# A hybrid attention and recurrence block: attention's output projection as seven block products, the gates' input sums by accumulating transfers, and fill work moved

## The chip, the cores and the metric

The kernel runs on one core of a Trainium2 chip. A core has five engines that run side by side and meet at semaphores: TensorE (PE in the profile; its weight loads are PEld), VectorE (DVE), ScalarE (ACT), GpSimd (POOL) and SyncE (SP). SP, ACT and POOL also issue transfers, each on a queue of its own (q1, q10 and q0 in the profile), which 16 DMA engines carry out. The metric is the time of one execution in device microseconds; lower is better.

## The reference

One layer of an encoder on x, 1024 tokens by 1024 channels, in float32:

```python
xn = rmsnorm(x, norm1_g)
u = xn @ w_in                                   # 1024 x 5632
q_sb, k_sb, v_sb, f_raw, i_hg, q_hg, g_hg, gate_sb, gate_hg = split(u)
o_sb = stick_breaking_attention(q_sb, k_sb, v_sb)      # 8 heads of 64: 512 wide
o_hg = hgrn2(silu(q_hg), (1 - lb) * sigmoid(-f_raw), i_hg, log_f)   # 4 heads of 128: 512 wide
o_hg = rmsnorm(o_hg, hg_norm_g) * silu(g_hg)
merged = sigmoid(gate_sb + b) * (o_sb @ w_o_sb) + sigmoid(gate_hg + b2) * (o_hg @ w_o_hg)
h = x + merged @ w_out
h = h + square(relu(rmsnorm(h, norm2_g) @ w_ff1)) @ w_ff2
out = rmsnorm(h, final_g)
```

The change is about `o_sb @ w_o_sb` (1024 x 512 by 512 x 1024) and about the operands of the products that give `gate_sb`, `gate_hg` and `g_hg`.

## The kernel before

*Products.* A float32 operand is split into a high part and a low part: `hi_lo` casts the high part on ScalarE (line 156) and subtracts on VectorE for the low part (line 161). A product is then three matmuls (`three`, line 570): high by high, high by low, low by high. Most matmuls have 512 columns.

*Seven products for eight.* The gates' projection, `w_out` and the MLP are multiplied as two-by-two blocks in Winograd's way: seven block products of sums of blocks in place of eight of the blocks themselves. The gates need their input xn in four blocks, whole (not split), added and subtracted, and each sum split again. `whole_input` (line 1455) makes a block whole in place, with an accumulating transfer on POOL's queue: low part += high part, 512 KB each. `sum_forms` (line 1461) then builds the sums for products 5, 6, 7 and 3 with additions on VectorE and splits them.

*Order of the work.* Each engine runs its instructions in one order that is fixed when the program is built. A planner makes that order: among the instructions that its own clock says are ready, it takes the one that stands first in the program, so an instruction can be issued well ahead of its place in the code. Buffers are handed out in the same way. Three things are written by hand. TensorE has two lanes: the main lane (attention's or the recurrence's own small products) and the fill lane (large projections, held as jobs in a stream `st`); a fill product may run at most two main blocks ahead (`open_block`, line 110). `st.advance` says how many steps of fill, six matmuls each, follow each piece of main work. And SP's loads are one chain in program order (`load`, line 135).

*The stages around the change.*

1. Attention, 64 items (8 heads x 8 query blocks). Fill: the projections of the heads, two raw jobs, and some of the recurrence's `f` and `q` projections, up to the job `j_att`. POOL's queue meanwhile builds sums of blocks of `w_out` in DRAM (`out_weight_sums`, line 1337). A finished head's output goes to DRAM (`od`).
2. The recurrence, four heads. `hg_levels` (line 1073) has 8 pieces a head, `hg_tail` (line 1214) 6; the tail of one head runs beside the levels of the next. Fill, so many steps a piece as `FILL` says (line 2434): the rest of the projections, then eight raw jobs (`raw_job`, line 1399, seven steps each) that compute, for each block of 128 gate columns, the two products of the gates that need no sums of xn, and load attention's output again (`osr`).
3. Attention's output projection, `sb_job` (line 1505): four jobs of two column blocks. For a column block and a token half, eight k-and-part products in 12 matmuls accumulate in one PSUM bank; the first half is multiplied by its gate, both are stored to `yd`. The first three jobs run beside the end of the recurrence and step `sum_forms` along; the fourth is held back and runs inside the first gate pair.
4. The gates, `gates` (line 1751): ten `GatePair`s, two of them for `g_hg`. Each runs `x6`, `y5`, `x7`, `y3`, four block products into two banks.

*Buffers.* 40 slots of 512 KB (`slot`), 10 of 256 KB (`half`), eight PSUM banks (`bank`), and of each of the weights' raw, high and low tiles two (`wpool`).

Of the kernel before, what the change touches and what calls it, by code (L numbers as in the profile page):

```python
# [2 lines left out]

# [36 lines left out]
def kernel(  # L40
# [972 lines left out]
    def silu_epilogue(h, key):  # L1013
        def ep(ps, half):
            t = hg_slot(h, key, half)
            ps, t = of_half(ps, half), as_half(t, half)
            nc.scalar.activation(t, ps, AF.Sigmoid)
            if h < 2:
                x = as_half(slot_n(f"qx{h}_{half}", 512), half)
                nc.scalar.copy(x, ps)  # L1020
                owed_wlo.append(lambda: mul(t, x, t))
                return
            mul(t, ps, t)

        return ep
# [282 lines left out]
    a_sb, a_hg = Split("asb"), Split("ahg")  # L1308
# [144 lines left out]
    WAIT = 7  # L1453
# [7 lines left out]
    def sum_forms():  # L1461


        raw = whole
        def split(m, kp, src):
            forms[m, kp] = tuple(slot(f"gs{n}{m}{kp}", F32R) for n in "hl")
            hi_lo(*forms[m, kp], src)

        for j in range(2):
            whole_input(0, j)  # L1470
        yield from range(WAIT)
        s1, s2 = {}, {}
        for kp in range(2):
            s1[kp] = slot(f"gs1{kp}")
            ins = add(s1[kp], raw[1, 0, kp], raw[1, 1, kp])
            if kp == 0:
                after(ins, hg_sum[0])
            yield
        for kp in range(2):
            split(5, kp, s1[kp])  # L1480
            yield
        for kp in range(2):
            s2[kp] = slot(f"gs2{kp}")
            sub(s2[kp], s1[kp], raw[0, 0, kp])
            yield
            split(6, kp, s2[kp])
            yield
        gates_in[0].load()
        gates_in[0].load_sums()
        for kp in range(2):  # L1490
            s3 = slot(f"gs3{kp}")
            sub(s3, raw[0, 0, kp], raw[1, 0, kp])
            split(7, kp, s3)
            yield
        gates_in[0].split()
        for kp in range(2):
            s4 = slot(f"gs4{kp}")
            sub(s4, raw[0, 1, kp], s2[kp])
            split(3, kp, s4)
            yield  # L1500
        gates_in[1].load()

    sb_units = []

    def sb_job(cp):
        src = W_OSB[:, cp * 256 : (cp + 1) * 256].rearrange("(k p) c -> p k c", p=P)
        unit = Unit(f"wo0{cp}", [[(0, 256, src)]])
        unit.roomy = (0,)
        sb_units.append(unit)

        def body():
            if cp == 0:
                side.append(sum_forms())
            for j in range(2):
                cb = 2 * cp + j
                if 1 < cb + 1 < KT:
                    load_g1(cb + 1)
                g1 = g1r[cb]
                for i, cs in halves():
                    ps = bank(f"pys{cb}_{i}")  # L1520
                    for _ in proj_half(
                        ps, unit.hl[0], a_sb.mov, 4, i, lambda k: k * 256 + j * P
                    ):
                        next(side[0], None)
                        yield
                    if i == 0:
                        mul(g1, ps, g1)
                        nc.gpsimd.dma_start(yd[cb][:, i, :], g1)
                    else:
                        y = half(f"ys{cb}")  # L1530
                        nc.scalar.copy(y, ps)
                        nc.scalar.dma_start(yd[cb][:, i, :], y)

        return st.add([unit], body)
# [12 lines left out]
    j_att = raw_job(KT + 1)  # L1547
    q_job(2)
    j_i = i_job()
# [3 lines left out]
    j_sb = [sb_job(cp) for cp in range(4)]  # L1553

    class GatePair:
# [3 lines left out]
        def load(self):  # L1559
            cb = self.cb  # L1560
            self.raw = [
                wpool.tile([P, 1024], F32, tag="raw", name=f"wg{cb}r{i}") for i in range(2)
# [26 lines left out]
        def split(self, behind=None):  # L1589
# [4 lines left out]
            after(sub(r0[:, s0], r0[:, s1], r0[:, s0]), first)  # L1594
            sub(r1[:, s0], r1[:, s1], r0[:, s0])
# [34 lines left out]
        def gate(self, t, which):  # L1630
            if self.cb < KT:
                nc.scalar.activation(t, t, AF.Sigmoid, bias=gate_bias(which, self.cb))
            else:
                s = half(f"gs{self.cb}")
                nc.scalar.activation(s, t, AF.Sigmoid)
                mul(t, t, s)
# [31 lines left out]
        def x7(self):  # L1668
# [4 lines left out]
            add(p14, p14, self.X)  # L1673
            self.gate(p1, 1)
# [76 lines left out]
    def gates():  # L1751
        for v, n, m in zip(gates_in, gates_in[1:] + [None], gates_in[2:] + [None] * 2):
# [8 lines left out]
            st.advance(SB_HELD.get(v.cb, 0), j_sb[3])  # L1761
# [4 lines left out]
            st.finish(j_sb[3])  # L1766
# [629 lines left out]
    n_fill = 9 * (NHS - 1 + 5) + 10  # L2396
    n_first = 4
    ready = deque()
    wsums = out_weight_sums()
    done = 0  # L2400
    for i, it in enumerate(items):
# [7 lines left out]
        if i % 2 == 1:  # L2409
# [18 lines left out]
    st.advance(1, j_q[2])  # L2428
# [25 lines left out]
    st.finish(j_sb[2])  # L2454
# [101 lines left out]
```

## Time and profile before

| | |
|---|---|
| median of 3 runs | 1420.13 us (1420.02 to 1420.27) |
| the profiled execution | 1420.01 us |
| its span, first to last instruction | 1418.2 us |
| TensorE busy | 1408.0 us, 99%, 6848 matmuls |
| VectorE busy | 1049.5 us, 74% |
| ScalarE busy | 659.3 us, 46% |
| GpSimd busy | 145.0 us, 10% |
| queue q1 (SP) | 192.48 MB, 41.0% of the 16 engines |
| queue q0 (POOL) | 34.61 MB, 9.9% |
| queue q10 (ACT) | 13.63 MB, 2.7% |

A busy TensorE is from the start of a matmul to its modelled end, and matmuls overlap; the time from one to the next is what a matmul costs. The "idle before" of a group of instructions tells how long its engine stood still just before it, and what ended that. The share of a queue is the time that its packets held the DMA engines. In a list of issues the last number is the time from issue to landing. Names are those of the program with the buffer's number left out: `xnl<-xnh` is a transfer that adds the high part of xn to its low part, `pys` the banks of attention's projection, `pga` and `pgq` those of the raw jobs, `pm`, `pX`, `pY` those of the MLP.

### The profile page before, as it was taken

To read this page: it belongs to the slowest core of one execution; us is meant where nothing else is said; L and a number is where in the kernel's file an instruction comes from. 1 tells how busy PE (TensorE), PEld (TensorE's weight loads), DVE (VectorE), ACT (ScalarE), POOL (GpSimd) and SP (SyncE) were. 2 spreads that over 40 slices of the span, in tenths; PEclk is the share of its full clock that TensorE was granted. 3 is DMA by queue.
4 is the path that set the end of the run, shared out by engine and by line. 5 is a ranking of instruction groups with operands and counts; after the bars stand their busy time and mean duration, and the time that the engine had idled before them with its cause. 6 is when DMAs were issued, how large, how long until landed. Compare 5 with 4: busy or idle time off the path is not lost.

```text
span 1418.2 us, 18602 instructions
## 1 busy us (share of the span) xinstructions
PE 1408.0 (99%) x6848; PEld 1183.5 (83%) x6848; DVE 1049.5 (74%) x1429; ACT 659.3 (46%) x1127; POOL 145.0 (10%) x282
## 2 busy tenths in 40 slices
PE   9999999999999999999999999999999999999998
PEld 7888888888888888888888888888888888888886
DVE  6667777778567888887788897676766657668765
ACT  6455555554243554433244764445444443534343
POOL 3011223110011031000000300000000000000042
PEclk9999999999999999999999999999999999999999
DMA  8344445435135685364585514444446974776725
GB/s 253 83 119 127 104 101 102 104 77 154 60 75 169 224 223 186 120 214 156 162 298 194 186 53 170 163 163 142 138 145 239 351 269 148 278 274 242 273 97 186
DMA packets 169730, 241.91 MB, mean 171 GB/s; under 512 B 30844, under 2 KB 97960, under 8 KB 169640
## 3 DMA queue, kind: packets, MB, share of 16 engines
q1 hardware_dynamic: 151432, 192.48, 41.0%
q0 software_dynamic: 11616, 34.61, 9.9%
q10 hardware_dynamic: 6592, 13.63, 2.7%
q8 instruction: 54, 0.88, 0.3%
q14 instruction: 36, 0.29, 0.1%
HBM read 170.43 MB, written 68.16 MB: 168 GB/s over the span
## 4 chain that ended last, share of the span: by engine, by line
PE 97%; ACT 1%; DMA 1%; DVE 1%; issue 0%; POOL 0%; SPq 0%; POOLq 0%; DVEq 0%; ACTq 0%
PE pm L128 21%; PE pX L128 9%; PE pW L128 6%; PE pY L128 6%; PE pjqk L128 6%; PE pga L128 4%; PE gX L128 4%; PE gY L128 4%; PE pjf L128 3%; PE pjq L128 3%; PE pys L128 3%; PE pji L128 3%; PE pyh L128 3%; PE po L128 3%; PE z L128 2%; PE pwX L128 2%
## 5 line engine op out<-in xcount | busy, mean ns | idle before, releaser
L854 DVE TENSOR_TENSOR_SCAN rm<-rm,bits 128x512 f32<-128x512 f32 (+6 forms) x72 | 87.5, 1222 | 30.5 <-ACT rm L835 29.0
L156 ACT CAST whid<-w 128x1024 fp32r<-128x1024 f32 x30 | 31.6, 1054 | 153.8 <-PE pm L128 85.4
L128 PE MATMUL pm<-wlod,sh 128*128 128x512 f32 x240 | 93.6, 390 | 0.0
L128 PE MATMUL pm<-whid,sl 128*128 128x512 f32 x240 | 93.5, 389 | 0.0
L128 PE MATMUL pm<-whid,sh 128*128 128x512 f32 x240 | 93.4, 389 | 0.0
L128 PE MATMUL pm<-tl,sh 128*128 128x512 f32 (+1 forms) x210 | 81.3, 387 | 0.0
L128 PE MATMUL pm<-th,sl 128*128 128x512 f32 (+1 forms) x210 | 81.3, 387 | 0.0
L128 PE MATMUL pm<-th,sh 128*128 128x512 f32 (+1 forms) x210 | 81.3, 387 | 0.0
L161 DVE TENSOR_TENSOR wlod<-w,whid 128x1024 fp32r<-128x1024 f32 x30 | 36.7, 1222 | 55.0 <-ACT whid L156 54.8
L156 ACT CAST wTh<-pw 128x512 fp32r<-128x512 f32 (+2 forms) x96 | 43.7, 482 | 62.4 <-PE pw L131 60.8
L161 DVE TENSOR_TENSOR wTl<-pw,wTh 128x512 fp32r<-128x512 f32 (+2 forms) x96 | 50.5, 548 | 28.9 <-ACT wTh L156 28.6
L161 DVE TENSOR_TENSOR sl<-sa,sh 128x1024 fp32r<-128x1024 f32 x56 | 68.2, 1218 | 0.6 <-ACT sh L156 0.6
L2173 POOL TENSOR_SCALAR fss<-fss 128x1 f32<-128x1 f32 x8 | 4.3, 543 | 562.0 <-ACT fsc L2168 561.5
L156 ACT CAST sh<-sa 128x1024 fp32r<-128x1024 f32 x56 | 57.2, 1045 | 7.8 <-DMA sa<-ad 7.8
L128 PEld LDWEIGHTS pm<-wlod,sh 128*128 128x128 f32 x240 | 45.1, 188 | 9.9 <-DVE wlod L161 0.4
L128 PEld LDWEIGHTS pm<-whid,sh 128*128 128x128 f32 x240 | 45.0, 188 | 9.4
L128 PEld LDWEIGHTS pm<-whid,sl 128*128 128x128 f32 x240 | 45.1, 188 | 9.2
L128 PE MATMUL pX<-sqh,t1l 128*128 128x512 f32 x128 | 50.0, 390 | 0.0
L128 PE MATMUL pX<-sql,t1h 128*128 128x512 f32 x128 | 50.0, 390 | 0.0
L128 PE MATMUL pX<-sqh,t1h 128*128 128x512 f32 x128 | 49.8, 389 | 0.0
L128 PEld LDWEIGHTS pm<-th,sh 128*128 128x128 f32 x210 | 39.5, 188 | 8.1
L128 PEld LDWEIGHTS pm<-tl,sh 128*128 128x128 f32 x210 | 39.4, 188 | 8.0
(936 smaller groups left out, 4358.8 us busy)
## 6 DMA issues: line engine op xcount, KB each, us to landing
w<-in_w_ff_dram SPq DMA_DIRECT2D x72, 512.0 KB, 4.8
sa<-ad SPq DMA_DIRECT2D x52, 512.0 KB, 6.8
ad<-a SPq DMA_DIRECT2D x32, 256.0 KB, 4.5
ad<-s SPq DMA_DIRECT2D x16, 512.0 KB, 3.2
tw<-in_w_out_dram POOLq DMA_DIRECT2D x24, 256.0 KB, 5.8
pr<-pd SPq DMA_DIRECT2D x10, 512.0 KB, 5.8
x<-in_x_dram SPq DMA_DIRECT2D x8, 512.0 KB, 7.9
xnl<-xnh POOLq DMA_DIRECT2D x8, 512.0 KB, 6.2
```

The costliest lines, as they stand in the source:

```text
L128: return pe(nc.tensor.matmul(*a, **k))
L156: hi_last[0] = after(in_turn("act", nc.scalar.copy(dst, src)), hi_behind[0])
L161: nc.vector.tensor_tensor(out=dst, in0=src, in1=hi.bitcast(F32), op=ALU.subtract),
L854: sc = nc.vector.tensor_tensor_scan(out=rr, data0=rr, data1=bits[:, 1024 - nk + a : 1024 - nk + b][:, ::-1], initial=rm[:, b : b + 1] if i ...
L2173: nc.gpsimd.tensor_scalar(out=ssq, in0=ssq, scalar1=1.0 / D, scalar2=EPS, op0=ALU.mult, op1=ALU.add)
```

## The change

*Attention's output projection.* The weights are taken as two-by-two blocks of 256 x 512, attention's output (channels by tokens) as blocks of 256 x 512. Seven block products, in the order 1, 6, 5, 7, 3, 4, 2, each of four column blocks of 128; a column block of a product is one step of fill, six matmuls. Products 1, 6, 7 and 4 accumulate in four banks, 5 and 3 in four others, 2 in four more later; copies on ScalarE and sums on VectorE are made between them. Six products are one job, behind the raw jobs; product 2 is the other, inside the first gate pair. The sums of weight blocks are made in DRAM, by eight more transfers on POOL's queue at the end of attention (`sb_weight_sums`). The sums of attended blocks are made by eight VectorE operations of 512 columns, in the steps of the last raw job (`sb_forms`); products 2 and 4 read their block from `od` again. A product's weights are loaded two products ahead and split one ahead.

*The gates' input sums.* `sum_forms` builds the sums of xn with eight accumulating transfers of 512 KB from SBUF to SBUF on POOL's queue, where there were eight VectorE additions. Only additions are possible so, so signs change in `raw_job`, `GatePair.split`, `x7` and `gate`. The first gate pair's raw weights go to slots.

*Fill.* `f_job(2)`, `q_job(1)` and `raw_job(KT + 1)` leave attention for the recurrence; `raw_job(KT)` and `q_job(0)` change places within it; `FILL` and the limits `upto` change.

```diff
-            if h < 2:
+            if h < 1:
                 x = as_half(slot_n(f"qx{h}_{half}", 512), half)
...
                 if k % 2 == 1:
+                    if cb == KT - 1:
+                        next(side[0], None)
                     yield
...
-            if 6 <= cb < KT:
-                load_g1(cb - 6)
-            if 5 <= cb < KT:
-                sb_units[cb - 5].load()
...
+            if cb == KT - 1:
+                sb_load(SB_ORDER[0])
+                side.extend((sb_forms(), sum_forms()))
...
-            add(p14, p1, p4)
+            sub(p14, p4, p1)
...
-            if 4 <= cb < KT:
-                a_sb.put(cb - 4, osb.pop(cb - 4))
...
     def sum_forms():
+        def split(m, i, j):
+            for kp in range(2):
+                forms[m, kp] = tuple(slot(f"gs{n}{m}{kp}", F32R) for n in "hl")
+                hi_lo(*forms[m, kp], whole[i, j, kp])
+                yield
+
+        def add_up(i, j, i2, j2):
+            for kp in range(2):
+                nc.gpsimd.dma_start(whole[i, j, kp], whole[i2, j2, kp], accum_op=ALU.add)
+                yield
+
+        yield from add_up(1, 1, 1, 0)
         for j in range(2):
             whole_input(0, j)
             yield
+        yield
+        yield from add_up(1, 0, 0, 0)
+        yield from split(5, 1, 1)
+        yield from add_up(0, 0, 1, 1)
+        yield
+        yield from split(7, 1, 0)
         gates_in[0].load()
         gates_in[0].load_sums()
+        yield
+        yield from add_up(0, 1, 0, 0)
+        yield from split(6, 0, 0)
+        gates_in[0].split()
+        yield
+        yield
+        yield from split(3, 0, 1)
...
+    SB_ORDER = (1, 6, 5, 7, 3, 4, 2)
...
+    def sb_form(m):
+        h, l = sb_s[m] = tuple(slot(f"as{n}{m}", F32R) for n in "hl")
+        if m in (2, 4):
+            c0 = 0 if m == 2 else 512
+            r = slot(f"asr{m}")
+            for kk in range(2):
+                load(r[:, kk * 512 : (kk + 1) * 512], od[2 + kk][:, c0 : c0 + 512])
+            hi_lo(h, l, r)
+            return
...
+        def end(m, cp, ps):
+            if m == 1:
+                sb_sum[cp] = slot(f"pu{cp}")
+                nc.scalar.copy(sb_sum[cp][:, 0:512], ps)
+            p1, u2 = (sb_sum[cp][:, cs] for _, cs in halves())
+            if m == 6:
+                nc.scalar.copy(u2, ps)
+            elif m == 7:
+                t = kept(ps, f"yt{cp}")
+                sub(t, sb_bank["Y", cp], t)
+                stored(cp + 4, 1, t, nc.gpsimd)
+                load_g1(cp + 4)
+            elif m == 3:
+                sub(u2, ps, u2)
+                gated(cp + 4, u2)
+            elif m == 4:
+                stored(cp, 1, kept(ps, f"yz{cp}"), nc.scalar)
+                load_g1(cp)
+            elif m == 2:
+                add(p1, p1, ps)
+                gated(cp, p1)
...
+            for m in order:
+                n = SB_ORDER.index(m)
+                ahead = SB_ORDER[n + 1 : n + 3]
+                for cp in range(4):
+                    end(m, cp, product(m, cp))
+                    if cp == 0 and ahead:
+                        sb_split(ahead[0])
+                        if len(ahead) > 1:
+                            sb_load(ahead[1])
+                    if cp == 1 and ahead:
+                        sb_form(ahead[0])
+                    if m == 4 and cp == 3:
+                        gates_in[1].load()
+                    next(side[0], None)
+                    yield
...
-        if h == 2:
+        if h == 3:
             raw_job(KT)
-        if h == 4:
-            q_job(0)
+    q_job(0)
     f_job(0)
     f_job(1)
+    j_att = j_f[1]
     q_job(1)
+    j_i = i_job()
     f_job(2)
-    j_att = raw_job(KT + 1)
     q_job(2)
-    j_i = i_job()
+    raw_job(KT + 1)
     f_job(3)
     q_job(3)
     j_raw = [raw_job(cb) for cb in range(KT)]
-    j_sb = [sb_job(cp) for cp in range(4)]
+    j_sb = [sb_job(SB_ORDER[:-1]), sb_job(SB_ORDER[-1:])]
...
-    n_fill = 9 * (NHS - 1 + 5) + 10
+    n_fill = 9 * (NHS - 1 + 3) + 3
...
-    wsums = out_weight_sums()
+    wsums = chain(out_weight_sums(), sb_weight_sums())
...
-        if i % 2 == 1:
+        if i % 2 == 1 or i % 8 == 0:
             next(wsums, None)
...
-    FILL = (3.4, 2.0, 2.6, 2.6, 2.9)
+    FILL = (3.6, 2.5, 2.8, 2.8, 3.0)
...
-        upto = (j_i, j_raw[1], j_raw[6], j_sb[1], j_sb[2])[h]
+        upto = (j_i, j_raw[0], j_raw[5], j_sb[0], j_sb[0])[h]
```

More of the change, by code (lines that the diff above doesn't have):

```diff
@@ L2 @@
 from contextlib import ExitStack
+from itertools import chain
 import concourse.bass as bass
@@ L1501, in sum_forms @@
[L1501 to L1509, printed above, removed]
-        def body():
[L1512 to L1534, printed above, removed]
+        yield
@@ new lines, in sb_weight_sums @@
+    def sb_weight_sums():
+        for t, op, src in (
+            (1, ALU.bypass, sb_block(0, 0)),
+            (3, ALU.bypass, sb_block(0, 1)),
+            (1, ALU.add, sb_block(0, 1)),
+            (3, ALU.add, sb_block(1, 1)),
+            (2, ALU.bypass, tv[1]),
+            (2, ALU.add, sb_block(1, 1)),
+            (4, ALU.bypass, tv[2]),
+            (4, ALU.add, sb_block(1, 0)),
+        ):
+            after(nc.gpsimd.dma_start(tv[t], src, accum_op=op), scored[0])
+            yield
@@ new lines, in sb_load, with sb_split @@
+    def sb_load(m):
+        plain = {1: (0, 0), 2: (1, 0), 3: (1, 1)}
+        sums = {5: 1, 7: 3, 6: 2, 4: 4}
+        src = sb_block(*plain[m]) if m in plain else tv[sums[m]]
+        sb_raw[m] = wpool.tile([P, 1024], F32, tag="raw", name=f"wo{m}r")
+        load(
+            sb_raw[m].rearrange("p (k c) -> p k c", k=2),
+            src.rearrange("(k p) c -> p k c", p=P),
+        )
+    def sb_split(m):
+        sb_w[m] = tuple(
+            wpool.tile([P, 1024], F32R, tag=t, name=f"wo{m}{t}") for t in ("whi", "wlo")
+        )
+        hi_lo(*sb_w[m], sb_raw.pop(m))
@@ new lines, in sb_forms @@
+    def sb_forms():
+        l, r = (cs for _, cs in halves())
+        pairs_ = ((osb[0], osb[2]), (osb[1], osb[3]))
+        sb_load(SB_ORDER[1])
+        sb_form(1)
+        yield
+        for a, b in pairs_:
+            sub(b[:, r], a[:, r], b[:, r])
+        yield
+        for a, _ in pairs_:
+            sub(a[:, r], a[:, l], a[:, r])
+        yield
+        for a, b in pairs_:
+            sub(a[:, l], b[:, r], a[:, l])
+        yield
+        for a, b in pairs_:
+            add(b[:, l], b[:, l], a[:, l])
+        yield
+        sb_split(1)
+        yield
@@ new lines, in sb_job, with product, kept, stored @@
+    def sb_job(order):
+        def product(m, cp):
+            open_block("fill")
+            (wh, wl), (sh, sl) = sb_w[m], sb_s[m]
+            name = {3: "Y", 5: "Y", 2: "W"}.get(m, "X")
+            start = m in (1, 5, 2)
+            if start:
+                sb_bank[name, cp] = bank(f"pys{name}{cp}")
+            ps = sb_bank[name, cp]
+            for k in range(2):
+                c = k * 512 + cp * P
+                ks = slice(k * 512, (k + 1) * 512)
+                three(
+                    ps, wh[:, c : c + P], wl[:, c : c + P], sh[:, ks], sl[:, ks],
+                    start and k == 0, k == 1, True,
+                )
+            return ps
+        def kept(ps, name):
+            t = half(name)
+            nc.scalar.copy(t, ps)
+            return t
+        def stored(cb, i, t, queue):
+            queue.dma_start(yd[cb][:, i, :], t)
+        def gated(cb, t):
+            g = g1r.pop(cb)
+            mul(t, t, g)
+            stored(cb, 0, t, nc.gpsimd)
+        def end(m, cp, ps):
[19 more added lines that the diff above has]
+                gated(cp, p1)
+        def body():
+            if order[0] == SB_ORDER[0]:
+                for _ in side[0]:
+                    pass
+                side.pop(0)
+            for m in order:
[12 more added lines that the diff above has]
+                    next(side[0], None)
+                    yield
+        made = Unit("sb", [])
+        made.late, made.hl = True, []
+        return st.add([made], body)
@@ L1561, in load @@
             self.raw = [
-                wpool.tile([P, 1024], F32, tag="raw", name=f"wg{cb}r{i}") for i in range(2)
+                slot(f"wg{cb}r{i}")
+                if self is gates_in[0]
+                else wpool.tile([P, 1024], F32, tag="raw", name=f"wg{cb}r{i}")
+                for i in range(2)
             ]
@@ L1672, in x7 @@
             add(p1, p1, self.X)
[L1673 to L1674 removed]
+            sub(p14, p14, self.X)
+            self.gate(p1, 1, -1.0)
             self.gate(p14, 0)
```

70 lines of the change are left out of this document (28 added, 42 removed).

## The prediction

> **What bounds the kernel now.** I read the page first (busy time, chain of waits), then what TensorE waited for, then the busy time by stage, and last the DMA engines around the attention output projection.
>
> ```profile
> span 1418.2 us, 18602 instructions
> PE 1408.0 (99%) x6848; PEld 1183.5 (83%) x6848; DVE 1049.5 (74%) x1429; ACT 659.3 (46%) x1127; POOL 145.0 (10%) x282
> PE 97%; ACT 1%; DMA 1%; DVE 1%; issue 0%; POOL 0%; SPq 0%; POOLq 0%; DVEq 0%; ACTq 0%
> ...
> PE warm L128 <- POOL ident masks.py:199: 2.3, 1, 2.3
> PE xnt L131 <- DVE x L653: 0.4, 1, 0.4
> ```
>
> TensorE is busy in 99% of the span, the chain that ended last is TensorE's for 97%, and its two longest waits, 2.3 and 0.4 us, lie at the start. So a matmul taken out is worth its issue time, and any new wait of TensorE is paid in full. The stages (columns: window, its length, busy time of PE, PEld, DVE, ACT, POOL with counts, clock, DMA share, GB/s):
>
> ```profile
> 960.00:1000.00 40.00, 40.00 (x178) 33.15 (x177) 27.96 (x38) 19.84 (x29) 0.00 (x0) 1.00 0.42 145
> 74.00:326.00 252.00, 251.94 (x1439) 218.12 (x1439) 183.79 (x239) 143.17 (x325) 54.64 (x133) 1.00 0.49 107
> 326.00:512.00 186.00, 186.00 (x993) 159.20 (x992) 138.80 (x238) 76.46 (x168) 20.04 (x28) 1.00 0.47 138
> 512.00:555.00 43.00, 43.00 (x232) 36.48 (x232) 36.08 (x50) 22.77 (x48) 8.61 (x12) 1.00 0.73 210
> 502.00:530.00 28.00, 28.00 (x152) 23.73 (x151) 23.52 (x36) 15.44 (x31) 8.51 (x11) 1.00 0.98 245
> ```
>
> The first row is a stretch of nothing but 512-column matmuls: 40.00 / 178 = 0.225 us from one to the next (the 390 ns that groups show overlap). The others are attention (74 to 326), the recurrence with its fill (326 to 512), and the stage with six of the eight column blocks of the attention projection (512 to 555). The last row is what decides this case: from 502 to 530 the DMA engines are busy at 0.98. TensorE rides through it (28.00 of 28.00), but there is no room left.
>
> **The saving.** Before, the projection is 8 column blocks x 2 token halves x 4 k x 3 = 192 matmuls; after, 7 block products x 4 column blocks x 2 k x 3 = 168. 24 x 0.225 = 5.4 us less, from 6848 matmuls to 6824.
>
> **The moved fill.** `f_job(2)`, `q_job(1)` and `raw_job(KT + 1)` leave attention for the recurrence: 48 + 48 + 36 = 132 matmuls, 29.7 us, so attention has 222 us where it had 252. Does it stay covered? A case near the tightest, the scan of an item and its transposes:
>
> ```profile
> 146.65 0.68 DVE L854 TENSOR_TENSOR_SCAN rm<-rm,bits 128x256 f32<-128x256 f32 x1
> ...
> 151.65 0.38 PE L131 MATMUL pw<-ident,rm 128*128 128x128 f32 x2
> ```
>
> The scan ends at 147.3, the transposes come at 151.7: 4.3 us to spare. An item becomes 0.46 us shorter (29.7 / 64), and it runs about two items ahead, so some 1 us of that goes. VectorE has 183.8 us to do, less some 11 us that moves with the jobs (four operations of 1024 columns at 1.22, ten of 512 at some 0.6), in 222: 78%. I take nothing lost, with 0 to 1.5 us as bounds. The recurrence gains cover: its TensorE was full (186.00 of 186.00) with less fill, so nothing either way. The eight added DRAM sums of weights sit on POOL's queue in the last fifth of attention; behind them on POOL wait the zeroing of the transposed tiles and the sums of the heads, due an item or more later: nothing.
>
> **VectorE and ScalarE in the stage.**
>
> ```profile
> L161 DVE TENSOR_TENSOR gsl<-gs,gsh 128x1024 fp32r<-128x1024 f32 x7 | 8.5, 1221 | 2.3 <-ACT gsh L156 2.3
> L169 DVE TENSOR_TENSOR g1r<-pys,g1r 128x512 f32<-128x512 f32 x6 | 4.1, 682 | 0.0
> L1314 DVE TENSOR_TENSOR gs<-xnl,xnl 128x1024 f32<-128x1024 f32 x2 | 2.4, 1220 | 0.0
> ```
>
> Out go eight additions of 1.22 (9.8 us). In come three more weight splits and three more forms (6 x 1.22 = 7.3), eight half-width sums of attended blocks and six more epilogue operations (14 x 0.68 = 9.5): 7 us more on an engine that had 36.08 of 43.00. By itself 0 to 4 us late at the first product, where the subtractions are queued ahead of the weights' low part; I put 0, because the next item covers it.
>
> **The transfers, where the price is.** Every input sum becomes an accumulating transfer of 512 KB on POOL's queue. The trace has two of exactly this form alone (418 to 427, DMA queues of that window):
>
> ```profile
> q0 software_dynamic: 288, 1.05, 61.8%
> ...
> xnl<-xnh POOLq DMA_DIRECT2D x2, 512.0 KB, 5.4
> ```
>
> 61.8% of 9 us for two: each holds all 16 engines for 2.78 us. Plain transfers, from 460 to 502:
>
> ```profile
> q1 hardware_dynamic: 6446, 5.69, 44.3%
> q10 hardware_dynamic: 1152, 2.10, 13.3%
> ```
>
> 44.3% of 42 us for 5.69 MB: 3.27 us per MB loaded; 13.3% for 2.10 MB: 0.70 us per 256 KB stored. And what happens to a load beside accumulations (516 to 526, then the issues from 500 to 556):
>
> ```profile
> q0 software_dynamic: 470, 1.61, 67.8%
> q1 hardware_dynamic: 634, 0.76, 23.2%
> q10 hardware_dynamic: 281, 0.52, 13.5%
> ...
> wo03r<-in_w_o_sb_dram SPq DMA_DIRECT2D x1, 512.0 KB, 16.7
> ```
>
> POOL's queue takes 68%, SP's loads get 23%; a 512 KB load of weights needed 16.7 us. It was due a whole job later, so nobody saw it.
>
> Now the stage after. Six such accumulations were there (4 of 1024-column `whole_input(0, ..)`, two of `whole_input(1, 1)`); eight `add_up` transfers join them, in a chain where each waits for the landing of the one before. By the planner's pace (steps of FILL: 1 + 28 + 35 + 40 + 39 = 143, the last raw job ends at 141) the first product starts as the levels of the last head end, and only `hg_tail(3)` runs beside it. Product 4 needs two operands loaded late: its form, from `od`, called for in product 3. SP's loads are one chain, so ahead of it stand five weight blocks (2.62 MB), four gates (1.05), the first gate pair with its stored parts (1.57) and the form itself (0.52): 5.76 MB.
>
> ```profile
> L128 PE MATMUL pga<-xnh,wga7whi x8: 388/390/476, 500.4 to 510.7; 128*128 128x512 f32 x8
> ...
> 502.12 0.92 POOL L1458 DMA_DIRECT2D xnl<-xnh  x1 [0.82 <-PE pga L128]
> ```
>
> *Time there is.* The first accumulation went out 1.7 us into the last raw job (500.4), that job ends 9 us later; 20 blocks of 6 matmuls are 27.0; `hg_tail(3)` has 37 matmuls at 0.12 ((43.0 - 144 x 0.225) / 88 others), 4.5. So product 4 is due 41 us after the first accumulation.
>
> *Work there is.* 14 x 2.78 = 38.9; 5.76 x 3.27 = 18.8; seven stores 4.9: 62.6 us of all engines, 64 at the share of 0.98. If the last two accumulations and product 7's four stores fall behind the form, 54.2, or 55. Then cast and subtraction, 1.05 + 1.22, and a hand-over: 3 us. Product 4 starts at 58 to 67, that is 17 to 26 us late, and everything on TensorE's fill lane is behind it. Earlier loads or gaps in the accumulations shorten it, a slower chain or full buffers lengthen it: bounds 9 to 30. I take 20, in the middle of the first pair and a little low, since each gap on POOL's queue lets a group of small loads through. While TensorE stands, the sums for the gates land, so `x6` and the rest cost nothing more.
>
> *Sum.* The profiled execution took 1420.01 us (span 1418.2; median of the runs 1420.13, the same to 0.01%): 1420.0 - 5.4 + 20 = 1434.6, say **1435 us**.
>
> The Trainium skill, in DMA: Bandwidth & Descriptors, section "Anatomy of one DMA — SWDGE (gpsimd) path", fits a transfer as 2.0 us fixed plus its bytes at 436 GB/s; 512 KB would hold the engines for 1.2 us. By that the work is 16.8 + 18.8 + 4.9 = 40.5, 44 with the split, the wait is 3 us, and the time 1418. The rows above say 2.78 us, more than twice that, and I go by them; it stays as part of the third case.
>
> **The rivals.** *The transfers keep up* (faster). The planner may issue loads long before the code names them, and before the change a 0.98 share cost TensorE nothing. If product 4's form lands within 38 us of the first accumulation, the saving is kept: 1420.0 - 5.4 + 0 to 1 = 1415. That takes 17 to 26 us less ahead of it, as much as all of SP's loads together (18.8), hence only 18%. *About even.* Either the form slips through and the chain to sum 6 ends last: 12 x 2.78 = 33.4 at 70 to 75% of the engines is 45 to 48, with its split 48 to 51, against `x6` due at 41 + 5.4 = 46: 2 to 5 us late. Or PSUM: products 1 and 5 hold four banks each of eight, and the two output banks of `hg_tail(3)` must pass between them, some 5 us for squares, root and product. Or the transfers are as quick as the page has them. 1417 to 1423: 16%. That attention runs dry would add at most 1.5 us and is within these.
>
> **How the numbers follow.** Forecast 66% (own range 1424 to 1446, from 9 to 30 us of wait), transfers keep up 18%, about even 16%. A measurement here can tell 0.2%, 2.8 us. Faster: 18% and a small part of the even case, 21%. Same: 11%. Slower: 66% and the upper end of the even case, 68%. The range 1415 to 1446 leaves out the lower half of the second case and the longest waits.
>
> **What would show it.** 6824 matmuls; 74 to 296 still full of TensorE. A wait of TensorE ended by the split of form 4 (`as..4`), or by a weight of a late product, with SP's load of it landing 15 us or more after its issue; POOL's queue at 60% or more of the engines for some 50 us; accumulations near 2.8 us of all engines each. Wrong if TensorE runs through the stage without a wait, or if it waits at `x6` or at a bank alone; wrong in size if the accumulations leave the engines free between them.

## The result, and the profile after

The changed kernel takes 1465.78 us (median of 4 runs, 1464.62 to 1467.51) beside 1420.15 in the same job: a ratio of 1.0322, 95% interval 1.0304 to 1.034. That is slower, as forecast, but 31 us above the 1435 foretold and above the range's end of 1446. The profiled run took 1465.0 us. First the page of the profile after, then the waits of TensorE, the stages (columns as before), and the DMA queues between 512 and 565.

```profile
span 1463.2 us, 18632 instructions
PE 1416.0 (97%) x6824; PEld 1185.4 (81%) x6824; DVE 1060.3 (72%) x1452; ACT 668.6 (46%) x1144; POOL 155.0 (11%) x302
PE 87%; DMA 4%; DVE 3%; issue 2%; ACT 2%; POOL 1%; SPq 0%; POOLq 0%; DVEq 0%; ACTq 0%
...
PE pysY L129 <- DVE k L1250: 8.6, 2, 7.4
PE pho L129 <- DVE hon L170: 7.0, 1, 7.0
PE gY L129 <- DVE pr L1315: 5.2, 2, 2.9
PE pysY L129 <- DVE yt L1318: 3.4, 1, 3.4
PE pysY L129 <- DVE hon L170: 3.4, 1, 3.4
PE sl L129 <- ACT ksl L1093: 2.6, 2, 1.3
...
PE po L129 <- DVE wTl L162: 2.1, 3, 1.0
PE pysX L129 <- ACT ash L157: 1.7, 1, 1.7
PE pysX L129 <- DVE asl L162: 1.6, 1, 1.6
...
74.00:300.00 226.00, 223.77 (x1313) 194.12 (x1312) 174.76 (x229) 134.97 (x313) 59.64 (x139) 1.00 0.59 126
520.00:540.00 20.00, 18.20 (x102) 15.28 (x100) 9.04 (x13) 12.70 (x22) 5.26 (x6) 1.00 1.06 254
540.00:560.00 20.00, 5.62 (x17) 3.92 (x18) 6.32 (x11) 5.97 (x15) 4.68 (x6) 0.72 0.99 216
560.00:580.00 20.00, 16.33 (x69) 13.32 (x68) 9.13 (x13) 6.63 (x16) 3.81 (x7) 0.85 0.62 189
...
q0 software_dynamic: 2176, 7.87, 76.0%
q1 hardware_dynamic: 3144, 3.83, 21.6%
```

There are 24 matmuls fewer, as said, but TensorE's chain is down from 97% to 87%, and between 540 and 560 it did 5.62 us of work. The DMA engines are as full as foretold (0.99 to 1.06; POOL's queue held 76.0% of 53 us = 40.3 us, the two stores of a raw job among it, against 38.9 worked out for 14 accumulations). But the wait is not where the prediction put it. Product 4's form (`ash`, `asl` into `pysX`) cost 3.3 us. The large waits stand ahead of it: 7.4, 7.0 and 3.4 us, and these end on the work of `hg_tail(3)`, the running state (`k`, line 1250) and the normed head (`hon`). (Smaller are 3.4 us for `yt`, the sum that reads product 5's bank before product 3 adds to it, and behind product 4 twice for `pr`, the gate's sum that reads `gY` before `y3` adds to it: 5.2.) What was the tail's work waiting for? The waits of ScalarE, VectorE and GpSimd between 515 and 565, then a piece of ScalarE's timeline and one of GpSimd's:

```profile
ACT gsh L157 <- DMA xnl<-xnl: 12.0, 4, 6.0
...
DVE gsl L162 <- ACT gsh L157: 10.1, 3, 4.9
DVE hon L170 <- POOL hn_y L270: 8.1, 1, 8.1
...
POOL xnl L1471 <- DMA xnl<-xnl: 20.5, 6, 8.2
...
546.35 1.04 ACT L157 CAST gsh<-xnl 128x1024 fp32r<-128x1024 f32 x1 [5.97 <-DMA xnl<-xnl]
...
548.73 0.28 ACT L1273 ACTIVATE hon<-pho 128x128 f32<-128x128 f32 x1
...
555.87 0.86 POOL L1471 DMA_DIRECT2D xnl<-xnl  x1 [3.19 <-DMA xnl<-xnl]
...
557.08 1.03 POOL L270 TENSOR_TENSOR hn_y<-hss,expo 128x4 f32<-128x4 f32 x1
```

`gsh` and `gsl` are the casts and subtractions of the gates' sums, `xnl<-xnl` the sums' transfers. The order on each engine is fixed, so while ScalarE waits 6.0 us for a sum to land, the tail's squares stand behind the cast: TensorE had written their bank (`pho`) by 537.3, and they came at 548.73. VectorE's state updates stand behind `gsl`, and GpSimd's powers `hn_y` behind issues of further sums, which wait for landings themselves: the squares were done at 549.9, the power came at 557.08. That is the theory (**queues in front**). Its rivals: PSUM **banks** (products 1 and 5 hold eight of them whatever the transfers do), **late operands** (the prediction's reason), and the **moved fill**.

### The profile page after: what moved, and what is told of

Same layout as the page of the kernel before. It is cut to its first block, busy times and chain, and to the rows that moved or that the text cites. A ratio compares the mean times of both kernels' runs of the same rounds, so it can differ in the third digit from the quotient of the medians.

```text
span 1463.2 us, 18632 instructions
## 1 busy us (share of the span) xinstructions
PE 1416.0 (97%) x6824; PEld 1185.4 (81%) x6824; DVE 1060.3 (72%) x1452; ACT 668.6 (46%) x1144; POOL 155.0 (11%) x302
## 4 chain that ended last, share of the span: by engine, by line
PE 87%; DMA 4%; DVE 3%; issue 2%; ACT 2%; POOL 1%; SPq 0%; POOLq 0%; DVEq 0%; ACTq 0%
PE pm L129 18%; PE pX L129 9%; PE pW L129 6%; PE pY L129 6%; PE pjqk L129 6%; PE gY L129 3%; PE gX L129 3%; PE pjq L129 3%; PE pji L129 3%; PE pjf L129 3%; PE pyh L129 3%; PE pga L129 3%; PE po L129 3%; PE z L129 2%; PE pwX L129 2%; PE pjv L129 2%
```

## The experiments

### The moved fill alone

The kernel before, with the jobs and paces of the kernel after and nothing else.

```diff
-            if h < 2:
+            if h < 1:
...
-    n_fill = 9 * (NHS - 1 + 5) + 10
+    n_fill = 9 * (NHS - 1 + 3) + 3
...
-    FILL = (3.4, 2.0, 2.6, 2.6, 2.9)
+    FILL = (3.6, 2.5, 2.8, 2.8, 3.0)
```

> The kernel before with the moved fill alone (two feature jobs, one query job and one raw job leave attention for the recurrence, the paces of the kernel after; the projection by column blocks and the gates' sums by VectorE as before; nothing left out). The prediction put 0 on this, with 0 to 1.5 us as bounds: 1420 to 1421.5. The trace after has the last product of attention 26.5 us earlier instead of 29.7: by that 3.2 us are lost in attention, and with some 1.5 us more in the recurrence, as in the run behind the tail, 1423 to 1425. If moved fill were the cause of the rest as well (waits in the projection stage), 1430 or more.

Measured: 1425.90 us (1425.62 to 1426.01), ratio 1.0042 (1.0027 to 1.0057): 6.0 us lost, more than either figure. TensorE's waits in it, none of which the kernel before shows:

```profile
PE sl L128 <- ACT ksl L1092: 2.6, 2, 1.3
...
PE po L128 <- DVE wTl L161: 2.1, 3, 1.0
```

The same two rows, with the same 2.6 and 2.1, stand in the kernel after. Attention's products (`po`) wait for attention weights of which the split is late, the recurrence's scores for a copy on ScalarE. No wait on the list accounts for the rest, some 1.3 us.

### The chain of sums: left out, by VectorE, and alone

Left out of the kernel after:

```diff
         def add_up(i, j, i2, j2):
             for kp in range(2):
-                nc.gpsimd.dma_start(whole[i, j, kp], whole[i2, j2, kp], accum_op=ALU.add)
                 yield
```

> The kernel after, with the eight accumulating transfers of add_up left out: the four sums of the input blocks of the gates' products are not formed, each product reads the plain block instead (the gates' values are another thing than the reference's). The six accumulations of the whole blocks stay, as in the kernel before, and so does every matmul, cast and subtraction. Head-of-line theory (the chain of sums fills the DMA engines, and the waits for its landings stand on ScalarE, VectorE and POOL in front of the work of hg_tail(3), which holds PSUM banks): the gap of TensorE between 541 and 563 (18.7 us) goes, and with it the lower clock after it; 1420 to 1430 us. Banks alone (products 1 and 5 hold eight banks beside hg_tail(3), whatever the transfers do): the gaps stay, 1455 us or more. Late operands of product 4 (the prediction): the gap before product 4 goes, but that is only 3.6 us of it: 1455 to 1462. Moved fill as the cause: nothing changes, 1465.

Measured: 1447.22 us (1446.23 to 1449.99), 18.6 less. By VectorE in its place (`add(t, whole[i, j, kp], whole[i2, j2, kp])` into a fresh slot):

> The kernel after, with the eight sums formed by VectorE into fresh slots (8 x 1.22 us, as before the change) where the eight transfers were; nothing is left out. Head-of-line theory: VectorE's sums end in 1.22 us each and nothing waits for a landing, so it is as without the chain, plus up to 9.8 us of VectorE in a stage where it then has little slack: 1422 to 1436 us. Banks alone: 1455 or more. If VectorE's own load in the stage is what holds the banks (its in-order queue, not the transfers), it comes out near or above the kernel after: 1460 to 1475.

Measured: 1448.63 us (1446.60 to 1450.93). So the chain costs some 18 us; VectorE's sums in its place cost 1.4, which is less than the spread of either kernel's runs. But 1447 is far from 1420 to 1430, and more is lost elsewhere. Now the chain alone, in the kernel before, with its projection by column blocks:

```diff
-            s1[kp] = slot(f"gs1{kp}")
-            ins = add(s1[kp], raw[1, 0, kp], raw[1, 1, kp])
...
+        yield from add_up(1, 1, 1, 0)
...
+        yield from add_up(1, 0, 0, 0)
+        yield from split(5, 1, 1)
```

> The kernel before with the gates' input sums by accumulating transfers alone (signs turned where the change turned them; projection by column blocks, fill as before; nothing left out). Chain and banks together as the cause: the column blocks hold at most two banks, so hg_tail(3) finds banks though its work is queued behind the sums' waits; 1417 to 1424 (ten sums of VectorE fewer). Chain alone as the cause of the stalls: TensorE waits in the tail as in the kernel after, 1435 or more. Saturated DMA engines (the prediction): the loads of the weights' columns are late, a wait for their split of 5 to 15 us, 1425 to 1435.

Measured: 1438.68 us (1438.35 to 1439.37), 18.8 more than before, the same price where no eight banks are held. TensorE's wait there, ScalarE's, and its queue at the place:

```profile
PE sl L128 <- ACT ksl L1092: 14.5, 2, 11.4
...
ACT gsh L156 <- DMA xnl<-xnl: 20.5, 4, 9.8
...
536.59 1.04 ACT L156 CAST gsh<-xnl 128x1024 fp32r<-128x1024 f32 x1 [7.22 <-DMA xnl<-xnl]
...
543.12 0.62 ACT L1092 COPY ksl<-k 128x512 f32<-128x512 f32 x1
```

The copy `ksl`, which the last levels' scores need, came at 543.12, behind casts that had waited 7.22 and 1.91 us for sums. Eight held banks are not needed for a loss of this size.

### Which queue

The transfers stay as they are and only the order changes. First the run above, with its casts behind the chain, the tail and the projection:

```diff
-        yield from split(5, 1, 1)
...
+        yield from range(20)
+        for m, i, j in ((6, 0, 0), (5, 1, 1), (7, 1, 0), (3, 0, 1)):
+            yield from split(m, i, j)
```

> The run with the gates' sums by transfers alone (1438.7), with the same transfers, but the casts and subtractions of the four summed forms queued behind the whole chain, hg_tail(3) and the projection, and not between the transfers; nothing left out. Queue in front: in that run ScalarE waited 9.8 and 7.2 us for landings with the copies of hg_levels(3) behind the cast; with the casts gone from there TensorE's wait of 14.8 us goes, and what is left is that the last sums land a little late for the gates (2 to 8 us): 1422 to 1429. DMA engines too busy (the prediction's reason): the transfers are the same, so the wait stays under this name or another: 1435 to 1440.

Measured: 1432.90 us (1432.02 to 1433.73): between the two expectations. The cast no longer stood in front, but a load did, on VectorE (its timeline):

```profile
530.90 0.69 DVE L1583 SCALAR_TENSOR_TENSOR wg8r<-wg8r,wg8r 128x512 f32<-128x512 f32 x1 [8.15 <-DMA wg8r<-in_w_in_dram]
531.51 0.68 DVE L169 TENSOR_TENSOR q<-q,pp 128x512 f32<-128x512 f32 x1
```

VectorE waited 8.15 us for a gate's weights. Their loads took 9.1 us from issue to landing, 4.9 before the change, while POOL's queue held 72.6% of the DMA engines (510 to 535). Behind them stood `q`, for which TensorE waited 5.2 us. The same edit in the kernel after:

> The kernel after, with the same move of the casts and subtractions behind the chain; nothing left out. If the queues of ScalarE and VectorE are what hold the tail's banks: the chain's price goes as when it is left out: 1446 to 1452. If GpSimd's queue holds them (the powers of hg_tail(3) behind the issues that wait for landings): the wait of 7.4 us for the bank of the head's output stays, 1455 to 1464. By the prediction (late operands): no change, 1463 to 1467.

Measured: 1467.20 us (1466.95 to 1467.47), no better. The time alone would fit the expectation for late operands, the trace does not: product 4 waited 1.7 us for its form, and the wait for the head's output bank (`pho <- hon`) grew to 23.6 us. GpSimd's timeline shows why; ScalarE's squares for it had ended at 546.2:

```profile
557.84 0.86 POOL L1471 DMA_DIRECT2D xnl<-xnl  x1 [4.04 <-DMA xnl<-xnl]
561.24 0.86 POOL L1471 DMA_DIRECT2D xnl<-xnl  x1 [2.54 <-DMA xnl<-xnl]
562.17 0.19 POOL L266 TENSOR_SCALAR hss<-hss 128x4 f32<-128x4 f32 x1
562.45 1.03 POOL L270 TENSOR_TENSOR hn_y<-hss,expo 128x4 f32<-128x4 f32 x1
```

A power of 1.03 us stood 16 us behind issues that waited for landings. So the last queue was cleared too: with the casts behind the chain, six of the eight accumulations follow the tail's two powers.

```diff
+                after(
                     nc.gpsimd.dma_start(whole[i, j, kp], whole[i2, j2, kp], accum_op=ALU.add),
+                    tail_powers[1] if (i, j) != (1, 1) else None,
+                )
```

> The kernel after, with the casts of the sums behind the chain (as in the run at 1467.2, where the wait for the head's output bank grew to 23.8 us while GpSimd's powers stood behind four more issues), and six of the eight accumulations issued behind the two powers of hg_tail(3) on GpSimd's queue; the same 14 transfers, nothing left out. Queues in front (ScalarE, VectorE and GpSimd all three): the tail runs through, its waits fall to the 5 us that were left without the chain; sums and form 4 come some us late: 1446 to 1455. DMA engines too busy, whatever the order: the same 18 us are lost elsewhere, 1462 to 1468.

Measured: 1447.38 us (1446.58 to 1448.15), the time of the kernel without the chain, with all 14 transfers. Its stages and TensorE's waits:

```profile
520.00:540.00 20.00, 20.00 (x111) 17.24 (x110) 11.78 (x20) 14.84 (x32) 4.76 (x6) 1.00 1.06 253
540.00:560.00 20.00, 16.11 (x68) 12.61 (x66) 6.90 (x9) 5.96 (x16) 5.81 (x8) 0.83 1.05 267
...
PE pysX L129 <- ACT ash L157: 8.3, 1, 8.3
...
PE pysY L129 <- DVE hon L170: 3.4, 1, 3.4
```

With the DMA engines at 1.06, TensorE ran 20.00 of 20.00, and 16.11 in the next 20 us, where the kernel after had 5.62. So the 18 us hang on the order in which the same transfers are issued and waited for, and not on their amount. Two limits belong to this. The order also moves transfers: between 540 and 560 POOL's queue now held 60.9% of the engines and SP's loads 43.3%, where the kernel after had 78.7% and 20.8%. And the load is not free: product 4's form cost 8.3 us here and 3.0 in the run without the chain, made up for by shorter waits elsewhere (`yt` 0.5 for 3.4, none for `pho` where there were 1.4). What remains of the tail is the rival with the banks: 3.4 us for `hon` (3.4 to 3.6 in every run where products stand beside the tail, none behind it). And now TensorE comes to product 4 in time to wait 8.3 us for its form: the step that the prediction named.

### The late form

Here the projection begins only behind the tail, with the transfers of the change.

```diff
-    FILL = (3.6, 2.5, 2.8, 2.8, 3.0)
+    FILL = (3.6, 2.5, 2.3, 2.3, 2.2)
...
-        upto = (j_i, j_raw[0], j_raw[5], j_sb[0], j_sb[0])[h]
+        upto = (j_i, j_raw[0], j_raw[5], j_raw[7], j_raw[7])[h]
```

> The kernel after, transfers as they are, but the pace of the fill is lowered (FILL 3.6, 2.5, 2.3, 2.3, 2.2 and a cap on the last two heads) so that the six raw jobs last through hg_tail(3) and product 1 starts only behind it; same work. Head-of-line and banks alike: with no tail beside the products no bank is held and nothing is queued behind the sums, so the gaps of 7.5, 7.4 and 3.8 us go. Late operands (the prediction): TensorE runs into product 4 with the chain still going, and waits there 9 to 20 us: about 1435. If the chain only hurts through the tail: 1417 to 1425. If the lower pace uncovers the recurrence, gaps appear in 330 to 500 instead.

Measured: 1459.02 us (1458.16 to 1459.96). Of the waits for the tail nothing is left, and the form is waited for (waits of TensorE, then ScalarE's timeline):

```profile
PE pysX L129 <- ACT ash L157: 17.0, 2, 12.5
...
576.99 1.04 ACT L157 CAST wo2whi<-wo2r 128x1024 fp32r<-128x1024 f32 x1 [15.61 <-DMA wo2r<-in_w_o_sb_dram]
581.03 1.04 ACT L157 CAST ash<-asr 128x1024 fp32r<-128x1024 f32 x1 [2.99 <-DMA asr<-od]
```

The longer of the two, 12.5 us, is product 4's; the other 4.5 are product 7's form, which the next expectation counts in by mistake. Even this is a queue in front: product 2's weights, not needed yet, stood ahead of product 4's form on ScalarE, which waited 15.61 us for their load; the form's own load cost 2.99 more. With the form loaded in the last raw job:

```diff
         sb_load(SB_ORDER[1])
+        for m in (4,):
+            od_load(m)
         sb_form(1)
```

> The run behind the tail, with the two loads of product 4's form issued in the last raw job, ahead of product 1's weights' split, and not in product 3; nothing else. In the run behind the tail TensorE waited 17.0 us for that form (12.5 and 4.5). If the form's load is late behind the chain and the loads ahead of it (the prediction's mechanism, where no tail hides it): the 12.5 us go, and 1443 to 1449 is left of 1459. If something else is late in product 4 (the weights' sum, the bank of product 7), only its name changes: 1454 to 1459.

Measured: 1453.21 us (1451.19 to 1455.45), 5.8 less and between the two expectations: product 4 no longer waited, while `yt` ahead of product 3 rose from 4.4 to 6.3 and the first gate's weights cost 3.3. The same edit on the run with the chain behind the powers:

> The run with the chain behind the powers of hg_tail(3) (1447.4), with the loads of product 4's form issued in the last raw job; nothing left out. TensorE waited 8.3 us for that form there. If the late load is the reason (the step of the prediction, at its place): the wait goes and 1438 to 1443 is left. If the wait moves to the next late load or form (the gates' weights, product 2's form): 1444 to 1448.

Measured: 1445.99 us (1445.68 to 1446.87), 1.4 less, as the second case has it; the 8.3 us for form 4 went and 5.4 for the gate's weights came. Here an operand made early moved the wait to the next one.

### What is left without chain, tail or late form

Sums by VectorE and the projection behind the tail (both edits above):

> Both of the above: the eight sums by VectorE and the projection stage behind hg_tail(3); nothing is left out. If head-of-line, banks and late operands are all there is: the saving of 24 matmuls is kept, 1415 to 1422 us. If the projection stage itself is bound by VectorE or ScalarE (three splits more, eight half-width sums), TensorE shows waits for weights' low parts or for forms there: 1425 or more. Banks alone predicts the same here as with the transfers behind the tail.

Measured: 1441.44 us (1440.19 to 1443.58), some 20 us above the first case: something in the projection stage itself is left. With the sums left out there:

> The run with sums by VectorE behind the tail (1441.4) with those eight sums left out (8 x 1.22 = 9.8 us of VectorE in the stage; the gates read plain blocks where sums belong, so their values are not the reference's). VectorE as the bound of the projection stage: most of 9.8 us goes with the clock that follows the waits: 1430 to 1436. If the waits there are for loads or banks: 1439 to 1443.

Measured: 1439.24 us (1438.97 to 1441.11); 9.8 us less of VectorE gave 2.2, so VectorE alone is not the bound here. With the sums on GpSimd (`nc.gpsimd.tensor_tensor` into fresh slots):

> The run with sums by VectorE behind the tail (1441.4), with the eight sums by GpSimd, nothing left out. VectorE as the bound and GpSimd quick enough: as with the sums left out, 1430 to 1437. If GpSimd's sums take several us each, or slow VectorE beside them: the forms come late, 1441 to 1450.

Measured: 1451.57 us (1451.24 to 1454.80), 10 worse. GpSimd's and VectorE's groups between 525 and 580, then three instructions in order of time:

```profile
L1472 POOL TENSOR_TENSOR gv<-xnl,xnl 128x1024 f32<-128x1024 f32 x4 | 11.6, 2908 | 3.6 <-DMA xnl<-xnh 3.4
...
L162 DVE TENSOR_TENSOR gsl<-gv,gsh 128x1024 fp32r<-128x1024 f32 x6 | 11.5, 1948 | 0.0
...
L162 DVE TENSOR_TENSOR wo7wlo<-wo7r,wo7whi 128x1024 fp32r<-128x1024 f32 x1 | 3.4, 3374 | 0.0
...
561.98 2.40 POOL L1472 TENSOR_TENSOR gv<-xnl,gv 128x1024 f32<-128x1024 f32 x1
562.57 0.69 DVE L1318 TENSOR_TENSOR pu<-pysY,pu 128x512 f32<-128x512 f32 x1 [1.44 <-PE pysY L129]
563.18 2.30 DVE L162 TENSOR_TENSOR wo4wlo<-wo4r,wo4whi 128x1024 fp32r<-128x1024 f32 x1
```

A sum takes GpSimd 2.9 us in the mean. VectorE's subtractions of two SBUF operands, 1.22 us elsewhere, took up to 3.37 beside one (the 1.95 is a mean of six `gsl`, of which two ran beside GpSimd's sums); the one with a PSUM operand at 562.57, inside a sum, took 0.69.

Three further edits of the run at 1441.4. Products 4 and 2 both left to the gates, form 4 loaded early:

```diff
-    j_sb = [sb_job(SB_ORDER[:-1]), sb_job(SB_ORDER[-1:])]
+    j_sb = [sb_job(SB_ORDER[:-2]), sb_job(SB_ORDER[-2:])]
```

> The run with sums by VectorE behind the tail (1441), with product 4's form loaded early as well, and products 4 and 2 left to the gates' first pair, four steps ahead of its third gate product and four behind it, as the last two column blocks were before the change (the second gate pair's raw weights get slots of their own for it); nothing left out. If cover in the gates and the late form are what is left: the waits of 2.4 us for the sum with gY in the first pair and of 3.7 us at product 4 go, with the lower clock behind them: 1428 to 1433. If VectorE's work in the stage is the bound, the waits only move: 1438 to 1444.

Measured: 1451.37 us (1450.53 to 1452.13): a miss; the gates waited 8.8 us for their first weights and product 2 waited 9.5 for its form. Product 2 between the third and fourth gate products (`SB_HELD = {KT: 0}`):

> The run with sums by VectorE behind the tail (1441.4), with the four blocks of product 2 between the third and fourth gate product of the first pair, and not ahead of the third; nothing left out. If the first gate pair lost the cover that two column blocks gave before the change: its wait of 2.4 us for the sum with gY goes, and the clock behind it: 1437 to 1439. If VectorE's backlog is the cause, the wait only moves: 1440 to 1443.

Measured: 1442.07 us (1441.92 to 1442.71), no gain, as the second case has it: the waits of 2.3 and 2.9 us for the sum with `gY` became one of 5.5. And that with the early form:

> The same, with the loads of product 4's form issued in the last raw job. If form 4 is late by its load: the waits of 1.9 and 2.1 us at product 4 go as well: 1433 to 1437. If by VectorE's and ScalarE's queues: no better than the run without the early load, within 2 us.

Measured: 1439.59 us (1438.72 to 1440.88), 2.5 less than without the early load and between the two expectations. Here VectorE is full (its busy time is the third after the window's length):

```profile
540.00:560.00 20.00, 16.25 (x70) 12.51 (x69) 20.00 (x23) 12.86 (x18) 2.56 (x5) 1.00 0.83 276
560.00:580.00 20.00, 17.39 (x68) 13.14 (x67) 19.08 (x24) 9.19 (x11) 1.82 (x4) 0.91 0.77 261
580.00:600.00 20.00, 15.96 (x71) 12.89 (x69) 20.00 (x29) 8.30 (x10) 2.16 (x4) 1.00 0.48 159
```

So 9.8 us were taken from it there:

> The run with sums by VectorE behind the tail, form 4 loaded early and product 2 between the gate products (1439.6), with the eight sums left out (the gates read plain blocks, so their values are not the reference's). In that run VectorE had hardly a pause from 537 to 603. VectorE as what bounds the stage once loads and queues are out of the way: most of 9.8 us goes, 1430 to 1434. If TensorE's waits there are for something else: 1437 to 1440.

Measured: 1435.49 us (1434.66 to 1435.89), 4.1 less and between the two expectations. From 540 to 580 VectorE now had pauses (busy 16.41 and 18.33 of 20 us); at the gates it was full still, and TensorE's longest wait stood (waits, then the stage):

```profile
PE gY L129 <- DVE pr L1315: 5.5, 1, 5.5
...
580.00:600.00 20.00, 14.54 (x60) 11.65 (x59) 19.90 (x30) 7.00 (x9) 2.16 (x4) 0.88 0.63 201
```

No version beats the kernel before: the best with nothing left out is 1439.59.

## Why the prediction was right and wrong

The direction held and the size did not. The runs split the 45.7 us between the two medians (1465.8 - 1420.1) so:

| part | us | from |
|---|---|---|
| 24 matmuls fewer | -5.4 | worked out in the prediction, 6848 to 6824 counted |
| moved fill | +6.0 | that change alone |
| sums' waits in front of the tail | +18.6 | kernel after less the one without the chain |
| projection beside the tail | +8.0 | without the chain: beside (1447.2) less behind (1439.2) |
| form 4 late, product 2's place | +3.8 | 1439.2 less 1435.5 |
| left over | +14.7 | 1435.5 less (1420.1 - 5.4 + 6.0) |

The split takes the parts away in one order, and another order could share them out differently. The runs at 1447.2, 1439.2 and 1435.5 leave out the eight sums, and the moved fill was measured in the kernel before, at another pace than in the runs behind the tail.

**The saving** was right in its count, 24 matmuls; no run measures its 5.4 us alone. **The transfers' work** was right too: 40.3 us of POOL's queue measured beside 38.9, SP's loads at 21.6% beside the 23% of before.

**What the full DMA engines do** is the step that failed. The prediction let TensorE run through `hg_tail(3)`, counted as 4.5 us of matmuls, and wait 20 us at product 4. It asked which operand of the *projection* is late, and not which instructions stand behind the waiting casts, subtractions and issues on ScalarE, VectorE and GpSimd. Those were the tail's, and TensorE stood still ahead of product 4, which then cost only 3.3 us. The named mechanism exists, a late form at product 4: 12.5 us with the tail out of the way (20 foretold), 8.3 with the queues cleared. It was hidden behind an earlier stall of the same origin. So "slower" came true by the waits for the sums' transfers, but not by the wait that carried the forecast, and in that the direction had some luck. That six accumulations cost TensorE nothing before was no evidence: between 500 and 560 neither ScalarE nor GpSimd waited for a landing there.

**The moved fill** at 0, with bounds of 0 to 1.5, was the second error: 6.0. The 4.3 us of slack came from one scan; the rows that waited were the splits of attention's weights (in the kernel after TensorE was busy 223.77 of the 226 us from 74 to 300), and the recurrence, taken as covered because it was full before, lost some of it as well.

**VectorE** at 0, "because the next item covers it", was the third. Seven more us were somewhat few: over the whole execution VectorE was busy 1060.3 us after the change and 1049.5 before, 10.8 more (the moved fill alone: 1049.7), in a stage that had become 5.4 us shorter. With the eight sums on VectorE as well (1067.4 in the run at 1439.6) it was busy 59.1 of the 60 us from 540; without them (the run at 1435.5) still 19.90 of 20 at the gates, and the gates' sums are late: `pr`, 5.2 us after the change, was in no rival.

**The rivals.** Banks were priced at some 5 us, instead of the forecast; measured, the wait for `hon` costs 3.4 of the 8.0 us beside the tail, on top of the rest. That transfers keep up (1415) fell with the first trace.

**Left open.** Of the 14.7 us, 9.5 are TensorE's waits in the run at 1435.5, most of them for VectorE (5.5 and 2.4); some 4 are slower matmuls behind waits (counted as in the last section); the rest is open. In that run the product that `pr` needs was done at 589.4, and `pr` came at 596.85, behind eight other operations of VectorE, the splits of the next pair's weights among them. Whether VectorE could be ordered so that the gates' sums are in time was not tried.

## What to carry to other kernels

Ask of every wait that a change adds what stands behind it on the same engine's queue, and follow those instructions to the PSUM banks and matmuls that need them: here that was worth 18 us with the same transfers, and changing the order alone gave it back. Saved matmuls are worth little when each brings casts, sums and splits to an engine that is nearly full in that stage (VectorE was busy 36.08 of 43.00 us before). A wait removed by an earlier load came back in part at the next late operand (5.4 us of 8.3 in one run), so sum the work of all the feeding engines over the stage before pricing one wait.

## What was not expected of the hardware

After a short wait TensorE can run at a lower granted clock. In the run with sums by VectorE behind the tail it waited 2.28 us, until 589.9, for the gate's sum; the stages around that, four us each:

```profile
588.00:592.00 4.00, 2.13 (x7) 1.75 (x8) 4.00 (x7) 1.04 (x2) 1.62 (x3) 0.85 1.00 283
592.00:596.00 4.00, 4.00 (x14) 3.15 (x14) 2.85 (x6) 0.98 (x3) 0.00 (x0) 0.72 0.81 312
596.00:600.00 4.00, 4.00 (x19) 3.29 (x18) 3.73 (x6) 2.33 (x3) 0.00 (x0) 1.00 0.04 17
```

With TensorE busy for all of it, the second row holds 14 matmuls where the third has 19; from 590.9 to 594.3 eight came some 0.43 us apart, not 0.225. In the kernel after, the 512-column matmuls between 505 and 660 that followed another such by 0.26 to 0.65 us are 45, in all 8.4 us above 0.225; before they were 12 with 1.1: by this estimate some 7 us of the loss is clock. In the run at 1435.5 they are 30 with 5.3. The Trainium skill, TensorE: Matmul & The Clock Gate, section "Part 1: The HAM clock gate", has the clock halve after a window of some 3.4 us without work; the halving agrees with 0.43 us, but here a wait of 2.28 us was enough.

That a GpSimd sum slows VectorE was not expected in this size, up to 3.37 us where 1.22 is usual. The Trainium skill, GPSIMD Engine Reference, section "Specifications", says that the two share their SBUF interfaces, with contention for VectorE instructions that have two SBUF inputs; the rows above agree, and the one with a PSUM operand kept its 0.69 us.
